# Value products with the values as stationary operand, two heads side by side, in three attention mixers

## The chip, the cores and the metric

The kernel runs on one core of a Trainium2 chip. The metric is the device time of one execution in microseconds. The core has TensorE (PE, matmuls; its weight loads are listed apart as PEld), VectorE (DVE), ScalarE (ACT), GpSimd (POOL) and SyncE (SP, which issues most DMAs). Matmul results land in PSUM banks, from which the other engines read.

## The reference

Two different transformer blocks of two layers each work on 512 tokens with 1024 features, in fp32. The first block has three mixers (sliding-window attention with sinks, HGRN2, mLSTM), the second has three attention mixers: a forgetting attention ("C", 6 heads of 64, a decay per head added to the scores), a differential one ("A", 4 heads of 64 from pairs of scores) and a dilated one ("B", 6 heads of 64). MLPs follow the mixers. The part that the change touches is, in the sliding-window mixer:

```python
    o = jnp.einsum('bnhgqk,bnkhd->bnqhgd', probs.astype(v.dtype), vv)
    return o.reshape(B, S, HQ * d)
```

and the like product of probabilities and values in mixers C and B. Each output is then multiplied by an output projection and added to the residual.

## The kernel before, in words

The residual x lies with features on the partitions, as 8 tiles of 128x512. A projection with weights is taken in three passes of split operands (`mm3`, L176 to L178): every operand is split into a high part and a rest by a ScalarE copy (L136) and a VectorE subtraction (L137). `feat_group` gives results with features on the partitions, `tok_group` with tokens on the partitions. The weights come by DMA from SP's queue.

The attention mixers go by token tiles t of 128 query rows. In mixers C and B a head's scores are one matmul of 64 rows (`softmax_block`, L1089: queries of the tile as stationary operand, keys moving); VectorE adds mask and maximum (L1093), ScalarE takes the exponential (L1094). `pv` (L1095 to L1107) transposes the probabilities in chunks of 128 keys (L1103, bank ps_T), copies them to at_pT (L1105), and then takes, for each chunk, the transposed probabilities (128x128) as stationary operand and 64 value columns as the moving one; the result goes to 64 columns of the bank ps_o, tokens on the partitions:

```python
        for c in range(t + 1):
            nc.tensor.matmul(po, pT[:, c * P:c * P + P], v(c), start=c == 0, stop=c == t)
```

After the last head of a tile one VectorE instruction multiplies ps_o by the reciprocal sums, broadcast over a head's 64 columns (L1164 in C into yc, L1231 in B into yo, L603 in `swa` into ysw). Before an output projection the results are brought to features on the partitions: by `to_feat` (L510 to L520, PE transposes L517, then a split) for ysw, yc and the differential mixer's ya, and by transposes at L1253 for yo. In `swa` two heads share a bank ps_T and one copy (L590 to L593) ahead of their value matmuls (L597). In mixer C, GpSimd loads the decay rows (fg_b, L1153) and adds the causal mask (L1154); the scores wait for that add.

Tile's scheduler sets the order of the instructions on each engine (`schedule_with_timeline_sim=True`, L1518) from the program order, the buffers and its own costs. The bank ps_o has one buffer, ps_T and ps_S two each, ps_mm three. The norms ahead of the next stage are generators whose pieces are woven in: `start` hands one over and `tick` advances it by the work done since (L216 to L236); `attend` in mixer B calls `tick(3000)` for each head.

Of the kernel before, what the change touches and what calls it, by code (L numbers as in the profile page):

```python
# [9 lines left out]
F32 = mybir.dt.float32  # L10
F32R = mybir.dt.float32r
BF16 = mybir.dt.bfloat16
I32 = mybir.dt.int32
# [48 lines left out]
class Builder:  # L62
# [328 lines left out]
    def mixers1(self, l, mp, act, nxt):  # L391
# [105 lines left out]
        sink = lambda m, pt, sl: nc.vector.tensor_tensor(self.x[m][:, sl], self.x[m][:, sl], pt, ALU.add)  # L497
        act = [self.to_feat(X, sub(ysw, i), "mm") for i in range(4)]
        for g in range(2):
# [23 lines left out]
    def swa(self, l, mp, sp, ysw, row):  # L523
# [44 lines left out]
        for t in range(NT):  # L568
# [9 lines left out]
            for j in range(8):  # L578
# [12 lines left out]
                if j % 2 == 1:  # L591
                    pT = sp.tile([P, S], F32, name="sw_pT", tag="sw_pT", bufs=2)
                    nc.scalar.copy(pT[:, :2 * w], tp[:, :2 * w])  # L593
                    for jj in (j - 1, j):
                        for c in range(w // P):
                            o, v = (jj % 2) * w + c * P, 640 + (jj % 2) * 64
                            nc.tensor.matmul(po[:, jj * 64:jj * 64 + 64], pT[:, o:o + P], ysw[k0 // P + c][:, v:v + 64],  # L597
                                             start=c == 0, stop=c == w // P - 1)
            nc.vector.tensor_tensor(es, sinks, mx, ALU.add)
            nc.scalar.activation(es, es, AF.Exp)  # L600
            nc.vector.tensor_tensor(den, den, es, ALU.add)
            nc.vector.reciprocal(den, den)
            nc.vector.tensor_tensor(ysw[t][:, 0:512].rearrange("p (h e) -> p h e", e=64),  # L603
                                    po.rearrange("p (h e) -> p h e", e=64),
                                    den.unsqueeze(2).broadcast_to([P, 8, 64]), ALU.mult)

# [490 lines left out]
    def pv(self, mp, s, t, po, v):  # L1097
# [8 lines left out]
        for c in range(t + 1):  # L1106
            nc.tensor.matmul(po, pT[:, c * P:c * P + P], v(c), start=c == 0, stop=c == t)  # L1107

    def mixers2(self, l, mp, act, nxt):
        nc = self.nc  # L1110
# [34 lines left out]
        for t in reversed(range(NT)):  # L1145
            po = self.ps("o")
            den = mp.tile([P, 6], F32, name="at_den", tag="at_den", bufs=2)
            for i in range(3):
                pair = []
                for h in (2 * i, 2 * i + 1):  # L1150
                    fbt = mp.tile([P, S], F32, name="fg_b", tag="fg_b", bufs=3)
                    w = (t + 1) * P
                    nc.gpsimd.dma_start(fbt[:, :w], fd[0, h * S:h * S + w].partition_broadcast(P))  # L1153
                    nc.gpsimd.tensor_tensor(fbt[:, t * P:w], fbt[:, t * P:w], self.c_caus[:, 3 * P:], ALU.add)  # L1154
                    pair.append(fbt[:, :w])
                ss = []
                for h in (2 * i, 2 * i + 1):
                    b = (h % 2) * 64
                    s, dn = self.softmax_block(mp, qk[i][b:b + 64], qk[3 + i][b:b + 64], t, pair[h % 2], 0.125)
                    nc.vector.reciprocal(den[:, h:h + 1], dn)  # L1160
                    ss.append(s)
                for h in (2 * i, 2 * i + 1):
                    self.pv(mp, ss[h % 2], t, po[:, h * 64:h * 64 + 64], lambda c: yc[c][:, h * 64:h * 64 + 64])
            nc.vector.tensor_tensor(yc[t][:, 0:384].rearrange("p (h e) -> p h e", e=64),  # L1164
                                    po[:, 0:384].rearrange("p (h e) -> p h e", e=64),
                                    den.unsqueeze(2).broadcast_to([P, 6, 64]), ALU.mult)

# [50 lines left out]
        sub = lambda y, i: [y[t][:, i * P:i * P + P] for t in range(NT)]  # L1218
        act = [self.to_feat(X, sub(yc, i)) for i in range(3)] + [self.to_feat(X, sub(ya, i)) for i in range(2)]

        def attend(t):
            po = self.ps("o")
            den = mp.tile([P, 6], F32, name="at_den", tag="at_den", bufs=2)
            for h in range(6):
                b = (h % 2) * 64
                s, dn = self.softmax_block(mp, qkb[h // 2][b:b + 64], qkb[3 + h // 2][b:b + 64], t,
                                           self.c_dil[:, (3 - t) * P:], 0.125)
                nc.vector.reciprocal(den[:, h:h + 1], dn)
                self.pv(mp, s, t, po[:, h * 64:h * 64 + 64], lambda c: yb[c][:, h * 64:h * 64 + 64])
                self.tick(3000)  # L1230
            nc.vector.tensor_tensor(yo[t].rearrange("p (h e) -> p h e", e=64),  # L1231
                                    po[:, 0:384].rearrange("p (h e) -> p h e", e=64),
                                    den.unsqueeze(2).broadcast_to([P, 6, 64]), ALU.mult)

# [6 lines left out]
        for sl in HALVES:  # L1241
# [3 lines left out]
            if wo is None:  # L1245
# [3 lines left out]
                aa = [(self.slot(Y, F32R), self.slot(Y, F32R)) for _ in range(3)]  # L1249
            for i in range(3):  # L1250
                pt = self.ps("T")[:, 0:S // 2]
                for u, t in enumerate(ts):
                    nc.tensor.transpose(pt[:, u * P:u * P + P], yo[t][:, i * P:i * P + P], self.ident)  # L1253
                self.split(aa[i][0][:, sl], aa[i][1][:, sl], pt)
            self.feat_group(wo, 3, 8, aa, sink, 0, (sl,))
# [267 lines left out]
```

## Time and profile before

| | |
|---|---|
| runs | median 2810.25 us of 3 (2807.56 to 2813.39) |
| profiled execution | 2809.55 us, its span 2807.8 us |
| PE busy | 2737.6 us (98%) |
| VectorE, ScalarE, GpSimd busy | 63%, 42%, 8% |
| DMA | 285.59 MB, mean 102 GB/s |

The span is the time from the first to the last instruction of the profiled execution. Busy shares are averages over the span. Matmuls are pipelined: the mean duration of one (some 270 ns for a small one) is longer than the time it takes from the engine, which is read from where the next one starts. A row of a timeline joins matmuls of one kind; its start is that of the first. A matmul with fp32 operands appears as two recorded passes. A shape such as 64*128 behind an operation is the part of the array it takes, rows by columns; 64x512 behind it is the moving operand. In rows of the order, the last shape is partitions by elements of the result's operand.

### The profile page before, as it was taken

How to read it: one execution, taken by the hardware profiler on the slowest of the kernel's cores; microseconds unless marked ns; L12 is line 12 of the kernel's file. 1: busy time of each engine (PE TensorE's matmuls, PEld its weight loads, DVE VectorE, ACT ScalarE, POOL GpSimd, SP SyncE). 2: the span in 40 equal slices, each digit the busy share in tenths (PEclk: the TensorE clock that was granted, in tenths of full speed). 3: DMA queues.
4: the chain of work that ended last, by engine and by line, in shares of the span. 5: the costliest groups of instructions: out<-in, count | busy, mean ns of one | idle time of the engine just before them, and what ended most of it. 6: DMA issues, size and time to landing. Idle time of an engine off the chain costs nothing.

```text
span 2807.8 us, 42599 instructions
## 1 busy us (share of the span) xinstructions
PE 2737.6 (98%) x16360; PEld 2343.3 (83%) x16360; DVE 1777.0 (63%) x3842; ACT 1174.7 (42%) x2294; POOL 235.8 (8%) x606
## 2 busy tenths in 40 slices
PE   8999999999999999999999999999999999999998
PEld 7887887889978788788988788888889777988887
DVE  7677777468667757766754656655554475665555
ACT  4644532226374543232634445433234544532332
POOL 2000100002200010000213100000000410000000
PEclk9998999999999999999999999999999999999999
DMA  4211486332221127733223121223332302133222
GB/s 153 76 48 52 136 263 226 103 104 92 90 72 46 54 98 254 256 130 102 91 83 112 30 72 57 89 86 98 99 105 81 100 23 86 39 105 98 90 89 77
DMA packets 87644, 285.59 MB, mean 102 GB/s; under 512 B 10972, under 2 KB 15132, under 8 KB 87440
## 3 DMA queue, kind: packets, MB, share of 16 engines
q1 hardware_dynamic: 81280, 266.49, 29.3%
q0 software_dynamic: 5872, 16.35, 2.2%
q8 instruction: 128, 2.10, 0.3%
q14 instruction: 76, 0.62, 0.1%
q10 hardware_dynamic: 288, 0.03, 0.0%
HBM read 280.69 MB, written 2.14 MB: 101 GB/s over the span
## 4 chain that ended last, share of the span: by engine, by line
PE 77%; DVE 9%; DMA 7%; issue 2%; ACT 2%; POOL 2%; SPq 0%; DVEq 0%; POOLq 0%; ACTq 0%
PE ps_mm L176 12%; PE ps_mm L177 12%; PE ps_mm L178 12%; DMA wm<-w_mod 5%; PE ps_T L176 5%; PE ps_T L177 5%; PE ps_T L178 5%; PE ps_S L176 5%; PE ps_S L177 5%; PE ps_S L178 5%; PE ps_S L1089 3%; PE ps_o L1107 2%; DVE wm L1032 2%; PE ps_T L1103 1%; DVE wl L137 1%
## 5 line engine op out<-in xcount | busy, mean ns | idle before, releaser
L136 ACT CAST wh<-wr 128x1024 fp32r<-128x1024 f32 (+4 forms) x414 | 407.2, 987 | 661.2 <-PE ps_mm L177 212.3
L137 DVE TENSOR_TENSOR wl<-wr,wh 128x1024 fp32r<-128x1024 f32 (+4 forms) x414 | 472.9, 1143 | 304.0 <-ACT wh L136 296.3
L177 PE MATMUL ps_mm<-slotA,wh 128*128 128x512 f32 (+1 forms) x632 | 229.3, 364 | 3.4 <-DVE slotA L317 2.0
L176 PE MATMUL ps_mm<-slotA,wh 128*128 128x512 f32 (+1 forms) x632 | 226.8, 366 | 1.5 <-ACT slotA L316 0.7
L178 PE MATMUL ps_mm<-slotA,wl 128*128 128x512 f32 (+1 forms) x632 | 226.7, 360 | 0.0
L176 PE MATMUL ps_mm<-wh,slotA 128*128 128x256 f32 (+3 forms) x688 | 207.6, 303 | 0.0
L177 PE MATMUL ps_mm<-wl,slotA 128*128 128x256 f32 (+3 forms) x688 | 206.2, 300 | 0.0
L178 PE MATMUL ps_mm<-wh,slotA 128*128 128x256 f32 (+3 forms) x688 | 205.6, 299 | 0.0
L1032 DVE CUSTOM_DVE_ANT_0 wm<-wm,sc 128x1024 f32<-128x1024 f32 x96 | 117.5, 1224 | 67.9 <-DMA wm<-w_mod 67.4
L136 ACT CAST m_h<-tmp 128x512 fp32r<-128x512 f32 (+1 forms) x122 | 71.4, 587 | 210.3 <-DVE tmp L911 173.9
L176 PE MATMUL ps_mm<-slotB,wh 128*128 128x512 f32 (+1 forms) x408 | 142.5, 359 | 2.6 <-ACT slotB L136 1.6
L177 PE MATMUL ps_mm<-slotB,wh 128*128 128x512 f32 (+1 forms) x408 | 143.6, 353 | 1.4 <-DVE slotB L137 1.4
L176 PEld LDWEIGHTS ps_mm<-wh,slotA 128*128 128x128 f32 x688 | 131.8, 192 | 12.1 <-issue 9.5
L178 PE MATMUL ps_mm<-slotB,wl 128*128 128x512 f32 (+1 forms) x408 | 141.7, 349 | 0.0
L177 PEld LDWEIGHTS ps_mm<-slotA,wh 128*128 128x128 f32 x632 | 122.4, 194 | 22.6 <-issue 3.1
L178 PEld LDWEIGHTS ps_mm<-wh,slotA 128*128 128x128 f32 x688 | 131.3, 191 | 12.0 <-issue 11.4
L176 PEld LDWEIGHTS ps_mm<-slotA,wh 128*128 128x128 f32 x632 | 121.6, 194 | 22.6 <-issue 3.6
L177 PEld LDWEIGHTS ps_mm<-wl,slotA 128*128 128x128 f32 x688 | 131.6, 191 | 10.2 <-issue 8.9
L178 PEld LDWEIGHTS ps_mm<-slotA,wl 128*128 128x128 f32 x632 | 122.5, 194 | 17.5 <-issue 2.6
L176 PE MATMUL ps_S<-m_h,wh 128*128 128x512 f32 (+1 forms) x355 | 129.8, 366 | 3.6 <-DVE yacc L945 3.3
L1094 ACT ACTIVATE at_s<-at_s,at_st 128x512 f32<-128x512 f32 (+3 forms) x160 | 89.5, 560 | 100.0 <-DVE at_st L1093 89.1
L178 PE MATMUL ps_S<-m_h,wl 128*128 128x512 f32 (+1 forms) x355 | 129.4, 365 | 0.0
(628 smaller groups left out, 7291.3 us busy)
## 6 DMA issues: line engine op xcount, KB each, us to landing
wr<-w_up SPq DMA_DIRECT2D x152, 512.0 KB, 3.8
wm<-w_mod SPq DMA_DIRECT2D x96, 512.0 KB, 4.6
wr<-w_dn SPq DMA_DIRECT2D x64, 512.0 KB, 4.0
wr<-w_dn SPq DMA_DIRECT2D x32, 384.0 KB, 3.1
wr<-w_dn SPq DMA_DIRECT2D x32, 320.0 KB, 2.9
wr<-w_f SPq DMA_DIRECT2D x16, 512.0 KB, 3.8
wr<-w_pg SPq DMA_DIRECT2D x16, 512.0 KB, 3.7
wr<-w_t SPq DMA_DIRECT2D x12, 512.0 KB, 4.9
```

The costliest lines, as they stand in the source:

```text
L136: nc.scalar.copy(hi, src)
L137: nc.vector.tensor_tensor(lo, src, hi.bitcast(F32), ALU.subtract)
L176: nc.tensor.matmul(out, ah, bh, start=i == 0, stop=False)
L177: nc.tensor.matmul(out, ah, bl, start=False, stop=False)
L178: nc.tensor.matmul(out, al, bh, start=False, stop=i == n - 1)
L1032: nc.vector.tensor_tensor_reduce(w, w, self.sc, 1.0, 0.0, ALU.mult, ALU.add, accum_out=self.mod[l][:, j:j + 1])
L1089: nc.tensor.matmul(pt, q[:, t * P:w], k[:, 0:w], start=True, stop=True, tile_position=None if row is None else (row, 0))
L1094: nc.scalar.activation(s, s, AF.Exp, bias=st[:, 0:1], scale=-1.0, accum_out=st[:, 1:2])
L1103: nc.tensor.transpose(tp[:, c * P:c * P + P], s[:, c * P:c * P + P], self.ident)
L1107: nc.tensor.matmul(po, pT[:, c * P:c * P + P], v(c), start=c == 0, stop=c == t)
```

## The change

`pv2` takes a pair of heads. It transposes both heads' probabilities and copies them, then takes for each chunk the values (128 keys x 64) as stationary operand and the transposed probabilities (128 keys x 128 tokens) as the moving one. The first head's result goes to partitions 0 to 63 of ps_o, the second's to 64 to 127 (`tile_position=(0, u * 64)`), so that the results have features on the partitions. `out_scaled` spreads the reciprocal sums over 64 columns a head (GpSimd, into tmp), transposes them into a bank ps_T, copies them back (ScalarE) and multiplies ps_o by them (VectorE). `parts_of` splits the results in pieces of 128x128 without transposes. Mixers C and B and `swa` use these; the differential mixer keeps `pv`. In B the transposes of the tail (L1253) go, the heads are taken in pairs, and `tick` is called once for each pair. Line numbers in the rows of the changed order are those of the changed file: L175 to L177 there are L176 to L178 before, L1086 is L1089, L580 is L581, L589 is L590, L1064 is L1067, L1186 and L1187 are L1153 and L1154.

```diff
@@ -495,7 +494,7 @@
 
         sub = lambda y, i: [y[t][:, i * P:i * P + P] for t in range(NT)]
         sink = lambda m, pt, sl: nc.vector.tensor_tensor(self.x[m][:, sl], self.x[m][:, sl], pt, ALU.add)
-        act = [self.to_feat(X, sub(ysw, i), "mm") for i in range(4)]
+        act = [self.parts_of(X, ysw, i) for i in range(4)]
         for g in range(2):
             self.feat_group(self.wload("w_oa1", l * 2 + g, 4 * 512), 4, 4, act, sink, 4 * g)
         self.hgrn_out(gg)
@@ -591,18 +590,16 @@
                 if j % 2 == 1:
                     pT = sp.tile([P, S], F32, name="sw_pT", tag="sw_pT", bufs=2)
                     nc.scalar.copy(pT[:, :2 * w], tp[:, :2 * w])
-                    for jj in (j - 1, j):
-                        for c in range(w // P):
-                            o, v = (jj % 2) * w + c * P, 640 + (jj % 2) * 64
-                            nc.tensor.matmul(po[:, jj * 64:jj * 64 + 64], pT[:, o:o + P], ysw[k0 // P + c][:, v:v + 64],
-                                             start=c == 0, stop=c == w // P - 1)
+                    for c in range(w // P):
+                        for u in range(2):
+                            o, v = u * w + c * P, 640 + u * 64
+                            nc.tensor.matmul(po[u * 64:u * 64 + 64, f * P:f * P + P], ysw[k0 // P + c][:, v:v + 64],
+                                             pT[:, o:o + P], start=c == 0, stop=c == w // P - 1, tile_position=(0, u * 64))
             nc.vector.tensor_tensor(es, sinks, mx, ALU.add)
             nc.scalar.activation(es, es, AF.Exp)
             nc.vector.tensor_tensor(den, den, es, ALU.add)
             nc.vector.reciprocal(den, den)
-            nc.vector.tensor_tensor(ysw[t][:, 0:512].rearrange("p (h e) -> p h e", e=64),
-                                    po.rearrange("p (h e) -> p h e", e=64),
-                                    den.unsqueeze(2).broadcast_to([P, 8, 64]), ALU.mult)
+            self.out_scaled(ysw[t][:, 0:512], po, den, 4)
 
 
     def hgrn(self, l, mp, yf, yhi):
@@ -1106,6 +1103,42 @@
         for c in range(t + 1):
             nc.tensor.matmul(po, pT[:, c * P:c * P + P], v(c), start=c == 0, stop=c == t)
 
+    def pv2(self, mp, ss, t, po, v):
+
+        nc = self.nc
+        w = (t + 1) * P
+        pTs = []
+        for s in ss:
+            tp = self.ps("T")
+            for c in range(t + 1):
+                nc.tensor.transpose(tp[:, c * P:c * P + P], s[:, c * P:c * P + P], self.ident)
+            pT = mp.tile([P, S], F32, name="at_pT", tag="at_pT", bufs=3)[:, :w]
+            nc.scalar.copy(pT, tp[:, :w])
+            pTs.append(pT)
+        for c in range(t + 1):
+            for u, pT in enumerate(pTs):
+                nc.tensor.matmul(po[u * 64:u * 64 + 64], v(c, u), pT[:, c * P:c * P + P], start=c == 0, stop=c == t,
+                                 tile_position=(0, u * 64))
+
+    def out_scaled(self, dst, po, rden, n):
+
+        nc = self.nc
+        pr = self.ps("T")
+        rb = self.tmp()[:, 0:n * P]
+        nc.gpsimd.tensor_copy(rb.rearrange("p (h e) -> p h e", e=64), rden.unsqueeze(2).broadcast_to([P, 2 * n, 64]))
+        for i in range(n):
+            nc.tensor.transpose(pr[:, i * P:i * P + P], rb[:, i * P:i * P + P], self.ident)
+        nc.scalar.copy(rb, pr[:, 0:n * P])
+        nc.vector.tensor_tensor(dst, po[:, 0:n * P], rb, ALU.mult)
+
+    def parts_of(self, which, ys, i):
+
+        h, lo = self.slot(which, F32R), self.slot(which, F32R)
+        for t in range(NT):
+            tt = slice(t * P, t * P + P)
+            self.split(h[:, tt], lo[:, tt], ys[t][:, i * P:i * P + P])
+        return h, lo
+
     def mixers2(self, l, mp, act, nxt):
         nc = self.nc
         X, Y = "A", "B"
@@ -1146,24 +1179,20 @@
             po = self.ps("o")
             den = mp.tile([P, 6], F32, name="at_den", tag="at_den", bufs=2)
             for i in range(3):
-                pair = []
+                pair, ss = [], []
                 for h in (2 * i, 2 * i + 1):
                     fbt = mp.tile([P, S], F32, name="fg_b", tag="fg_b", bufs=3)
                     w = (t + 1) * P
                     nc.gpsimd.dma_start(fbt[:, :w], fd[0, h * S:h * S + w].partition_broadcast(P))
                     nc.gpsimd.tensor_tensor(fbt[:, t * P:w], fbt[:, t * P:w], self.c_caus[:, 3 * P:], ALU.add)
                     pair.append(fbt[:, :w])
-                ss = []
                 for h in (2 * i, 2 * i + 1):
                     b = (h % 2) * 64
                     s, dn = self.softmax_block(mp, qk[i][b:b + 64], qk[3 + i][b:b + 64], t, pair[h % 2], 0.125)
                     nc.vector.reciprocal(den[:, h:h + 1], dn)
                     ss.append(s)
-                for h in (2 * i, 2 * i + 1):
-                    self.pv(mp, ss[h % 2], t, po[:, h * 64:h * 64 + 64], lambda c: yc[c][:, h * 64:h * 64 + 64])
-            nc.vector.tensor_tensor(yc[t][:, 0:384].rearrange("p (h e) -> p h e", e=64),
-                                    po[:, 0:384].rearrange("p (h e) -> p h e", e=64),
-                                    den.unsqueeze(2).broadcast_to([P, 6, 64]), ALU.mult)
+                self.pv2(mp, ss, t, po[:, i * P:i * P + P], lambda c, u: yc[c][:, (2 * i + u) * 64:(2 * i + u) * 64 + 64])
+            self.out_scaled(yc[t][:, 0:384], po, den, 3)
 
         qka = [self.slot(Y) for m in range(4)]
         for g in range(2):
@@ -1216,21 +1245,22 @@
         w = self.wload("w_bv2", l, 8 * 384, parts=4)
         self.tok_group(w, 8, 384, act, lambda t, pt: nc.scalar.copy(yb[t], pt))
         sub = lambda y, i: [y[t][:, i * P:i * P + P] for t in range(NT)]
-        act = [self.to_feat(X, sub(yc, i)) for i in range(3)] + [self.to_feat(X, sub(ya, i)) for i in range(2)]
+        act = [self.parts_of(X, yc, i) for i in range(3)] + [self.to_feat(X, sub(ya, i)) for i in range(2)]
 
         def attend(t):
             po = self.ps("o")
             den = mp.tile([P, 6], F32, name="at_den", tag="at_den", bufs=2)
-            for h in range(6):
-                b = (h % 2) * 64
-                s, dn = self.softmax_block(mp, qkb[h // 2][b:b + 64], qkb[3 + h // 2][b:b + 64], t,
-                                           self.c_dil[:, (3 - t) * P:], 0.125)
-                nc.vector.reciprocal(den[:, h:h + 1], dn)
-                self.pv(mp, s, t, po[:, h * 64:h * 64 + 64], lambda c: yb[c][:, h * 64:h * 64 + 64])
-                self.tick(3000)
-            nc.vector.tensor_tensor(yo[t].rearrange("p (h e) -> p h e", e=64),
-                                    po[:, 0:384].rearrange("p (h e) -> p h e", e=64),
-                                    den.unsqueeze(2).broadcast_to([P, 6, 64]), ALU.mult)
+            for i in range(3):
+                ss = []
+                for h in (2 * i, 2 * i + 1):
+                    b = (h % 2) * 64
+                    s, dn = self.softmax_block(mp, qkb[i][b:b + 64], qkb[3 + i][b:b + 64], t,
+                                               self.c_dil[:, (3 - t) * P:], 0.125)
+                    nc.vector.reciprocal(den[:, h:h + 1], dn)
+                    ss.append(s)
+                self.pv2(mp, ss, t, po[:, i * P:i * P + P], lambda c, u: yb[c][:, (2 * i + u) * 64:(2 * i + u) * 64 + 64])
+                self.tick(6000)
+            self.out_scaled(yo[t], po, den, 3)
 
         yo = [self.slot(X)[:, 0:384] for t in range(NT)]
         wo = None
@@ -1247,11 +1277,10 @@
                     self.feat_group(self.wload("w_oa2", l * 4 + g, 5 * 256), 5, 2, act, sink, 2 * g)
                 wo = self.wload("w_ob2", l, 3 * 1024, parts=3)
                 aa = [(self.slot(Y, F32R), self.slot(Y, F32R)) for _ in range(3)]
-            for i in range(3):
-                pt = self.ps("T")[:, 0:S // 2]
-                for u, t in enumerate(ts):
-                    nc.tensor.transpose(pt[:, u * P:u * P + P], yo[t][:, i * P:i * P + P], self.ident)
-                self.split(aa[i][0][:, sl], aa[i][1][:, sl], pt)
+            for t in ts:
+                tt = slice(t * P, t * P + P)
+                for i in range(3):
+                    self.split(aa[i][0][:, tt], aa[i][1][:, tt], yo[t][:, i * P:i * P + P])
             self.feat_group(wo, 3, 8, aa, sink, 0, (sl,))
             self.start(nxt(sl))
```

**First place:** PE in mixer C of the first layer of the second block, at the last token tile, where ps_o takes value products, ps_T transposes, ps_S scores, and ps_mm is a projection woven in. Before:

```order
L176 MATMUL ps_mm<-wh,slotA 128x256
L1107 MATMUL ps_o<-yc_14478,at_pT 128x64
L1107 MATMUL ps_o<-yc_14479,at_pT 128x64
L1107 MATMUL ps_o<-yc_14480,at_pT 128x64
L1107 MATMUL ps_o<-yc_14481,at_pT 128x64
L1103 MATMUL ps_T<-ident,at_s 128x128 x4
L1089 MATMUL ps_S<-slotB 128x512 x2
L177 MATMUL ps_mm<-wl,slotA 128x256
```

The same place in the changed program:

```order
L177 MATMUL ps_mm<-wh,slotA 128x256
L1120 MATMUL ps_o<-at_pT,yc_14550 64x128
L1120 MATMUL ps_o<-at_pT,yc_14551 64x128 x2
L1120 MATMUL ps_o<-at_pT,yc_14552 64x128 x2
L1120 MATMUL ps_o<-at_pT,yc_14553 64x128 x2
L1114 MATMUL ps_T<-ident,at_s 128x128 x4
L1120 MATMUL ps_o<-at_pT,yc_14550 64x128
L1114 MATMUL ps_T<-ident,at_s 128x128 x4
L1086 MATMUL ps_S<-slotB 128x384 x2
```

The two heads' matmuls of a chunk now follow each other, in a run of seven; the eighth, the first head's first, had gone ahead, as it does for the next pair: alone, between the transposes of that pair's two heads.

**Second place:** PE in `swa` of the first layer of the first block, at a token tile with two chunks of keys. Before:

```order
L177 MATMUL ps_mm<-wl,slotA 128x264
L597 MATMUL ps_o<-ysw_205,sw_pT 128x64 x2
L581 MATMUL ps_S<-sw_q_765,slotB 128x256
L178 MATMUL ps_mm<-wh,slotA 128x264
L590 MATMUL ps_T<-ident,sw_s 128x128 x2
```

The same place in the changed program:

```order
L176 MATMUL ps_mm<-wl,slotA 128x264
L580 MATMUL ps_S<-sw_q_765,slotB 128x256
L596 MATMUL ps_o<-sw_pT,ysw_205 64x128 x2
L596 MATMUL ps_o<-sw_pT,ysw_206 64x128 x2
L177 MATMUL ps_mm<-wh,slotA 128x264
L175 MATMUL ps_mm<-wh,slotA 128x264
L589 MATMUL ps_T<-ident,sw_s 128x128 x2
```

Here the four value matmuls of a pair of heads stand together, chunk by chunk.

**Third place:** POOL in mixer C, where fg_b is the decay row of a head and rp_a belongs to the differential mixer's rotary embedding. Before:

```order
L1153 DMA fg_b<-fg_d_14626 128x384
L1154 TENSOR_TENSOR fg_b<-fg_b,c_caus 128x128 x2
L1153 DMA fg_b<-fg_d_14626 128x384 x2
L1067 TENSOR_TENSOR rp_a<-rp_a,rp_b 128x256
L1154 TENSOR_TENSOR fg_b<-fg_b,c_caus 128x128 x2
```

The same place in the changed program:

```order
L1186 DMA fg_b<-fg_d_14698 128x384
L1187 TENSOR_TENSOR fg_b<-fg_b,c_caus 128x128
L1128 COPY tmp<-at_den 128x384
L1187 TENSOR_TENSOR fg_b<-fg_b,c_caus 128x128
L1186 DMA fg_b<-fg_d_14698 128x384 x2
L1064 TENSOR_TENSOR rp_a<-rp_a,rp_b 128x256
```

The copy that spreads the reciprocals of one token tile stands between the mask adds for the next.

## Rows read from the trace of the kernel before

**Rows 1.** The page: busy time by engine, and the last chain by engine.

```profile
PE 2737.6 (98%) x16360; PEld 2343.3 (83%) x16360; DVE 1777.0 (63%) x3842; ACT 1174.7 (42%) x2294; POOL 235.8 (8%) x606
...
PE 77%; DVE 9%; DMA 7%; issue 2%; ACT 2%; POOL 2%; SPq 0%; DVEq 0%; POOLq 0%; ACTq 0%
```

**Rows 2.** Waits of PE: what, on whom: us in total, times, longest.

```profile
PE ps_S L176 <- ACT wh L136: 9.8, 3, 7.6
...
PE ps_o L1107 <- ACT at_pT L1105: 0.7, 2, 0.3
```

**Rows 3.** Groups of instructions on PE: xcount, busy us, mean ns, idle before.

```profile
L1107 PE MATMUL ps_o<-yb,at_pT 128*128 128x64 f32 x240 | 32.5, 271 | 1.0 <-ACT at_pT L1105 0.7 <-DVE slotA L1231 0.3
L1107 PE MATMUL ps_o<-yc,at_pT 128*128 128x64 f32 x240 | 29.8, 269 | 0.0
L597 PE MATMUL ps_o<-ysw,sw_pT 128*128 128x64 f32 x224 | 29.0, 270 | 0.0
```

**Rows 4.** Chain that ended last, mixer B: start us, us, what.

```profile
1686.78 1.29 PE ps_o L1107 x12
```

**Rows 5.** Timeline of PE in hgrn: start us, us, instruction, xcount.

```profile
172.53 0.39 PE L679 MATMUL ps_o<-yhi,hg_kt 128*128 128x128 f32 x2
172.75 0.49 PE L789 MATMUL ps_T<-ident,yg 128*4 128x128 f32 x3
```

**Rows 6.** Timeline of PE, 64x64 tiles in a long run and alone.

```profile
198.26 1.30 PE L733 MATMUL ps_S<-tmp 64*64 64x64 f32 x34
...
201.59 0.33 PE L733 MATMUL ps_S<-tmp 64*64 64x64 f32 x2
```

**Rows 7.** Timeline of PE around one transpose of four rows.

```profile
190.25 0.28 PE L176 MATMUL ps_mm<-wh,slotA 128*128 128x256 f32 x1
190.46 0.22 PE L811 MATMUL ps_T<-ident,ml_P 4*128 4x4 f32 x1
...
190.84 0.28 PE L178 MATMUL ps_mm<-wh,slotA 128*128 128x256 f32 x1
```

**Rows 8.** Timeline of PE around one transpose onto six columns.

```profile
1486.12 0.28 PE L176 MATMUL ps_mm<-wh,slotA 128*128 128x256 f32 x1
1486.24 0.28 PE L177 MATMUL ps_mm<-wl,slotA 128*128 128x256 f32 x1
1486.36 0.27 PE L1130 MATMUL ps_o<-ident,yc 128*6 128x128 f32 x1
1486.39 0.37 PE L177 MATMUL ps_mm<-wl,slotA 128*128 128x256 f32 x1
1486.59 0.28 PE L178 MATMUL ps_mm<-wh,slotA 128*128 128x256 f32 x1
```

**Rows 9.** Timelines of PE around score products L1089 in mixer B.

```profile
1671.71 0.39 PE L176 MATMUL ps_mm<-slotA,wh 128*128 128x512 f32 x1
1671.94 0.39 PE L177 MATMUL ps_mm<-slotA,wh 128*128 128x512 f32 x1
1672.26 0.70 PE L1089 MATMUL ps_S<-slotB 64*128 64x256 f32 x2
...
1673.22 0.39 PE L176 MATMUL ps_mm<-slotA,wh 128*128 128x512 f32 x1
...
1710.21 1.12 PE L1089 MATMUL ps_S<-slotB 64*128 64x512 f32 x2
...
1722.51 1.13 PE L1089 MATMUL ps_S<-slotB 64*128 64x512 f32 x4
```

**Rows 10.** Groups on GpSimd and ScalarE: xcount, busy us, mean ns, idle before.

```profile
L1067 POOL TENSOR_TENSOR rp_a<-rp_a,rp_b 128x256 f32<-128x256 f32 x40 | 32.8, 822 | 241.0 <-DVE rp_b L1066 153.7 <-DVE df_c L1194 41.0 <-PE ps_S L1089 18.6
L1154 POOL TENSOR_TENSOR fg_b<-fg_b,c_caus 128x128 f32<-128x128 f32 x48 | 22.1, 463 | 52.3 <-DMA fg_b<-fg_d 51.6
L1105 ACT COPY at_pT<-ps_T 128x384 f32<-128x384 f32 x32 | 14.6, 475 | 19.5 <-PE ps_T L1103 19.5
```

**Rows 11.** Busy time in a window: us, PE, PEld, DVE, ACT, POOL, PEclk, DMA, GB/s.

```profile
1698.20:1708.40 10.20, 10.20 (x35) 7.40 (x36) 2.79 (x12) 3.27 (x11) 0.00 (x0) 0.50 0.08 28
```

More of the change, by code (lines that the diff above doesn't have):

```diff
@@ L11 @@
 F32R = mybir.dt.float32r
-BF16 = mybir.dt.bfloat16
 I32 = mybir.dt.int32
```

## Prediction

> **What bounds the kernel now.** I read the page first [rows 1]: PE is busy 2737.6 of the span's 2807.8 us, VectorE 63%, ScalarE 42%, GpSimd 8%, and 77% of the chain that ended last lies on PE. Then PE's waits [rows 2]: the longest group is 9.8 us in the whole run, and the value matmuls waited for their transposed probabilities for 0.7 us in all. So the kernel issues on PE nearly all the time, and an edit is worth what it saves or adds in PE's own stream, unless it makes a new wait. The value matmuls of the three mixers are 240, 240 and 224 recorded passes [rows 3], 704 in all (two passes to one fp32 matmul). Their mean of 270 ns is the latency of one; they overlap. The price of a pass is its share of a stretch: twelve took 1.29 us on the chain [rows 4], 0.1075 each.
>
> **Removed: the old value passes.** 704 x 0.1075 = **-75.7 us**. A pass streams only 64 columns but holds a full 128x128 stationary operand.
>
> **Added: the new value passes.** The orders hold the same 352 matmuls, so 704 passes, now with a 128x64 stationary and 128 moving columns. A pass of 128 moving columns alone costs 0.11: two L679 passes lead to the next row 0.22 us later [rows 5] (172.53 to 172.75). Two heads stand side by side in the array. No row shows that shape, the nearest is the hgrn product L733, 64x64 tiles: two lone passes take 0.33 us, 34 passes take 1.30 [rows 6], so the other 32 add 0.97, 0.030 each, against 0.1075 for a full-array pass of 64 columns. Passes on different tiles therefore run beside one another. With two column tiles I take half, 0.056 a pass: 704 x 0.056 = **+39.4**. Bounds: 0.053 (half of 0.1075) and 0.11 (no overlap, a rival below).
>
> **Passes without a partner.** The changed order on PE hoists the first matmul of head 0 to where its probabilities are copied, before head 1 is there (first order place of the change). I count 119 runs of 128x64 tiles: 32 in the sliding-window mixer, 24 of four and 8 of two, all paired (second place), and 87 in the second block: 47 of one matmul and 31 others of odd length (12 of three, 10 of five, 9 of seven). 78 matmuls thus have no partner; each costs a half more on its two passes, 2 x 0.055 = 0.11: **+8.6**.
>
> **Lost pairs of score products.** L1089 takes 64 rows; two neighbours on different row halves run together: at 512 columns four passes take 1.13 us and two take 1.12 [rows 9]. By the order the pairs go from 50 to 40 (64 rows) and from 8 to 6 (32 rows), 12 pairs less, so 12 excursions more. One at 256 columns: from 1671.94 to 1673.22 are 1.28 us over two steps that take 0.23 each (1671.71 to 1671.94) [rows 9], 0.82. 12 x 0.8 = **+9.6**; between 0.4 (at 128 columns, the product itself being a third) and 1.1 (512 columns) 5 to 13.
>
> **Fewer excursions in hgrn.** The scheduler groups the 64x64 products better: 33 entries from the full array become 18. What one costs is seen at L811, a transpose of 4 rows among 128-row matmuls: from L176 at 190.25 to L178 at 190.84 are 0.59 us [rows 7], for two steps of 0.12 (1486.12 to 1486.24, [rows 8]); 0.35, of which I leave 0.02 to its own four columns. 15 x 0.33 = **-5.0** (-5 to 0, as the order on the chip may wait elsewhere).
>
> **Transposes.** 80 go (24 and 32 of L517, 24 of L1253), 80 come (spread reciprocals), all 128x128: **0** on PE.
>
> **The new chain behind each token tile.** Before, one VectorE multiply emptied the bank ps_o. Now, 24 times, a GpSimd copy spreads the reciprocals, PE transposes them, ScalarE copies them back, then VectorE multiplies. GpSimd took 463 ns for an add at 128x128 and 822 at 128x256 [rows 10], 0.36 per further 128 columns, so about 1.2 us at 128x384 (an estimate; a copy has one input less); the ScalarE copy took 0.475 [rows 10]. The bank and its result come 1.65 us later. In the forgetting mixer the copies also stand in GpSimd's queue between the loads of fg_b and the mask adds (third place), where the next tile's scores wait for those adds. If all 24 stood on the path, 24 x 1.65 = 40; if PE has other work, 0. PE's queue puts weight matmuls between, and the like hand-over today costs 0.7 [rows 2]; the places with least cover are the ends of the two dilated halves in each of two layers. I take **+4**, two to three of the 24.
>
> **At nothing.** ScalarE gets 24 copies (24 x 0.475 = 11 us [rows 10]), and it and VectorE the splits as 80 pieces of 128x128 in place of 26 larger ones: the same elements in more instructions. ScalarE is at 42%, VectorE at 63%, and PE's stream covers both; without that cover the dilated ends would show it, within the term above. No DMA is added or removed; SP issues the same transfers with a few neighbours swapped, so the weights come as before. The tick per pair moves the pre-norm pieces by half a pair, no work.
>
> **Sum.** -75.7 + 39.4 + 8.6 + 9.6 - 5.0 + 4 = -19.1. The profiled execution took 2809.55 (0.7 below the median of 2810.25), so 2790.4; I forecast **2790 us**. This case's own range is 2780 (no new wait, cheap lost pairs) to 2802 (nine tiles' chains exposed).
>
> **Does a change of columns drain the array?** The order counts 661 changes of the array's shape between matmuls, 465 before. In this trace the drain shows where the number of rows changes [rows 7, 9]. Where only columns change it does not: the transpose onto 6 columns at 1486.36 between two weight matmuls [rows 8] makes 1486.24 to 1486.59 last 0.35 instead of 0.24, and 0.11 is the price of its own 128 moving columns; L789 onto 4 columns stands beside L679 at 0.11 a pass [rows 5]. I take no drain for 128x64. But those rows ask for 6 and 4 columns at column 0 of the array; nothing shows a tile that begins at column 64.
>
> **Rival 1, slower: the column tiles drain like the row tiles.** Of the 119 runs' ends, 95 entries come from the full array and 113 exits go to it (the rest border on row tiles, which drain anyway): 208 switches, 104 trips x 0.33 = +34.3, so -19.1 + 34.3 = +15: **2825** (2815 to 2832, at 0.24 to 0.40 a trip). The gain is gone from 0.18 a trip. For it: a tile that begins at column 64 is as much a tile of its own as one that begins at row 64. Against it: [rows 5, 8]. Chance 0.28.
> The Trainium skill, page "TensorEngine Tiling (Array Packing)", section Tiling Modes, lists 128x64 as a mode of its own and says that "changing tiling mode (not just tile) drains the TensorE"; by that rule this rival's sum holds, and the trace agrees for rows and does not for fewer columns at column 0.
>
> **Rival 2, the change does not do what it says:** the column tiles don't run side by side. Then 704 x 0.11 = 77.4 stands in place of 39.4 + 8.6, 29.4 more: +10, about **2820**, without drains. For it: only tiles that differ in rows also take different partitions of the moving operand; here both take all 128. Against it: 0.030 in [rows 6] is nearer a quarter of 0.1075 than a half, so columns too run beside each other there. Chance 0.05.
>
> **Rival 3: the new chain decides.** Half of the 24 tiles expose their 1.65 us, 20 in place of 4, and the stretch at half clock in the dilated second half (10.2 us at 0.50 [rows 11]) grows by the pauses: about **2808**. For it: one ps_o bank, GpSimd in a row with DMA issues. Against it: the scheduler placed other PE work between. Chance 0.07.
>
> **How the numbers follow.** Main case 0.60. A measurement here tells about 0.2% from no change, 5.6 us: 2804 to 2816. Faster: nearly all of the main case and a bit of rival 3, 0.59. Same: rival 3, the main case's upper end and rival 1's lower, 0.10. Slower: rivals 1 and 2, 0.31. The range 2778 to 2826 holds the main case, rivals 2 and 3 and over half of rival 1.
>
> **What would show it.** Right: value rows 64x128 in runs of four passes lasting about 0.22 us beyond one pass; weight matmuls around them at their usual step plus the passes' share; waits of PE on ps_T behind GpSimd or on ps_o of a few us in all. Rival 1: 0.3 us more around each run. Rival 2: passes 0.11 apart in both halves. Rival 3: "POOL tmp" or "DVE yc" high among PE's waits. The forecast is wrong if the weight matmuls around a run are late by more than the passes explain.

## The result and the profile after

The changed kernel took 2878.93 us (median of 4 runs, 2875.6 to 2879.35) where the kernel before took 2809.65: 1.0242 times, 95% interval 1.0225 to 1.026. It is 69 us slower. The forecast was 2790, its range ended at 2826, and the dearest rival stood at 2825.

The page of the changed kernel, busy time by engine, against [rows 1]:

```profile
PE 2780.4 (97%) x16360; PEld 2345.0 (82%) x16360; DVE 1781.7 (62%) x3896; ACT 1194.1 (42%) x2372; POOL 247.8 (9%) x630
...
PE 78%; DVE 9%; DMA 6%; ACT 3%; POOL 2%; issue 2%; SPq 0%; DVEq 0%; ACTq 0%; POOLq 0%
```

Nothing here names a cause: PE is busy 43 us more with as many passes. The span and the mean granted clock of TensorE do, before and then after:

```profile
core 0: 2807.8 us, clock 0.984
```

```profile
core 0: 2877.1 us, clock 0.965
```

Span times (1 - clock) is 44.9 us before and 100.7 after. Up to 56 of the 69 us are therefore PE at its lower level of 1.2 GHz. Where it was is shown by the page's line of 40 slices of 72 us: two dips to 5, where the line of the kernel before has one slice at 8 and none lower:

```profile
PEclk9995999999999589999999999999999999999999
```

The first is the hgrn and mLSTM part of the first layer. Windows there, after (us, busy PE, PEld, DVE, ACT, POOL, PEclk, DMA share, GB/s):

```profile
210.00:230.00 20.00, 13.62 (x220) 11.78 (x221) 19.84 (x44) 6.87 (x11) 2.56 (x4) 0.80 0.25 81
230.00:250.00 20.00, 15.77 (x159) 11.74 (x156) 15.22 (x24) 10.06 (x22) 0.00 (x0) 0.50 0.00 1
250.00:270.00 20.00, 20.00 (x74) 15.57 (x73) 3.96 (x8) 6.92 (x18) 2.42 (x4) 0.50 0.09 26
270.00:290.00 20.00, 17.24 (x66) 14.31 (x65) 12.29 (x47) 7.57 (x22) 0.69 (x1) 0.50 0.00 1
```

The same stretch before, from 20 us earlier on:

```profile
190.00:210.00 20.00, 17.07 (x276) 15.45 (x274) 19.84 (x44) 7.61 (x12) 2.85 (x4) 1.00 0.26 83
210.00:230.00 20.00, 20.00 (x131) 15.60 (x130) 14.61 (x22) 8.85 (x16) 0.00 (x0) 0.83 0.16 53
230.00:250.00 20.00, 20.00 (x110) 15.46 (x110) 11.70 (x21) 12.29 (x29) 2.44 (x4) 1.00 0.24 79
```

VectorE is busy 19.84 of 20 us in hgrn, before and after. What PE did ahead of the fall of the clock, in the first layer (L177 is a weight pass, L676 and L730 are hgrn's):

```profile
217.66 0.39 PE L177 MATMUL ps_mm<-slotA,wl 128*128 128x512 f32 x1
217.89 0.38 PE L676 MATMUL ps_o<-yhi,hg_kt 128*128 128x128 f32 x2
218.64 0.76 PE L730 MATMUL ps_S<-tmp 64*64 64x64 f32 x18 [0.37 <-DVE slotB L737]
```

The weight pass at 217.66 us is followed by none until 292.8. The clock fell to 0.5 at 222.1 us, after 1.0 us of idle time from 218 on, and stayed there for 72 us; most of the 6.4 us that PE idled in the first window came after the fall. In the second layer the weight passes pause from 945.4 to 1026.1 us, and the clock is at 0.5 for 78 us from 949.1 on. Whether the want of work took the clock down is tested below. PE's waits (us in all, times, longest) show hgrn's products L730 and the mLSTM's L865 and L853, where the kernel before waited 0.5 us at the first of these lines (L733 there), 0.5 at the second (L868) and not at the third:

```profile
PE ps_S L730 <- DVE slotB L737: 8.2, 4, 5.9
...
PE ps_S L730 <- DVE slotA L737: 7.7, 4, 6.0
...
PE ps_T L865 <- DVE ml_P L860: 5.5, 2, 2.8
PE ps_S L853 <- DVE ml_P L860: 4.3, 2, 2.2
PE ps_T L1130 <- POOL tmp L1128: 4.2, 1, 4.2
```

The last line is the new spread chain: one wait of 4.2 us. Why hgrn came late is seen on VectorE. Its preparation begins with an operation into a tmp buffer (L635 before, L632 after). Before, then after:

```profile
70.36 0.69 DVE L635 SCALAR_TENSOR_TENSOR tmp<-slotB 128x512 f32<-128x512 f32 x1
```

```profile
160.11 0.20 DVE L601 RECIPROCAL sw_den<-sw_den 128x8 f32<-128x8 f32 x1
160.23 0.64 DVE L632 SCALAR_TENSOR_TENSOR tmp<-slotB 128x512 f32<-128x512 f32 x1
```

It moved by 90 us, to right behind the reciprocals of the last token tile of `swa`. The order says what follows: with 123 of hgrn's 274 matmuls issued, 163 weight passes were still to come before the mLSTM's last product in the kernel before; after, 14 were left, and none from hgrn's 133rd matmul on. PE had spent its filling work while hgrn waited.

The new value passes themselves, in mixer C (start us, us, xcount), against a 0.12 step of the weight passes [rows 8]:

```profile
1577.31 0.28 PE L176 MATMUL ps_mm<-wl,slotA 128*128 128x256 f32 x1
1577.43 0.28 PE L177 MATMUL ps_mm<-wh,slotA 128*128 128x256 f32 x1
1577.64 1.09 PE L1120 MATMUL ps_o<-at_pT,yc 128*64 128x128 f32 x14
1578.66 0.44 PE L1114 MATMUL ps_T<-ident,at_s 128*128 128x128 f32 x2
```

Entry takes 0.21 instead of 0.12. In the trace partners start 0.007 us apart and pairs 0.109 apart. The 14 passes are six pairs and one matmul without a partner, whose two passes take a step each: eight steps, 0.87. From 1577.43 to 1578.66 are 1.23, so 0.24 is left behind the weight pass's 0.12; and the second transpose starts 0.164 behind the first instead of 0.109. The trip to the column tiles and back thus costs 0.29, the drain that [rows 7] show for rows at about the same price. The 59 runs of the trace that stand at full clock between full-array passes, with a pass of 128 columns behind, have a median of 0.29. A run of four among weight passes of 256 columns in `swa`:

```profile
90.71 0.28 PE L175 MATMUL ps_mm<-wh,slotA 128*128 128x256 f32 x1
90.92 0.44 PE L596 MATMUL ps_o<-sw_pT,ysw 128*64 128x128 f32 x4
91.29 0.39 PE L176 MATMUL ps_mm<-wl,slotA 128*128 128x256 f32 x1
91.51 0.28 PE L177 MATMUL ps_mm<-wh,slotA 128*128 128x256 f32 x1
```

0.80 from 90.71 to 91.51, less 0.24 for the two weight passes and 4 x 0.0545 for two pairs, leaves 0.34.

### The profile page after: what moved, and what is told of

It is laid out like the page before. It is cut to its first block, busy times and chain, and to the rows that moved or that the text cites. A ratio compares the mean times of both kernels' runs of the same rounds, so it can differ in the third digit from the quotient of the medians.

```text
span 2877.1 us, 42842 instructions
## 1 busy us (share of the span) xinstructions
PE 2780.4 (97%) x16360; PEld 2345.0 (82%) x16360; DVE 1781.7 (62%) x3896; ACT 1194.1 (42%) x2372; POOL 247.8 (9%) x630
## 4 chain that ended last, share of the span: by engine, by line
PE 78%; DVE 9%; DMA 6%; ACT 3%; POOL 2%; issue 2%; SPq 0%; DVEq 0%; ACTq 0%; POOLq 0%
PE ps_mm L175 12%; PE ps_mm L177 12%; PE ps_mm L176 12%; DMA wm<-w_mod 5%; PE ps_T L175 5%; PE ps_T L176 5%; PE ps_T L177 5%; PE ps_S L175 5%; PE ps_S L177 5%; PE ps_S L176 5%; PE ps_S L1086 3%; DVE wm L1029 2%; PE ps_o L1120 2%; PE ps_T L1114 1%; PE ps_S L580 1%
## 5 line engine op out<-in xcount | busy, mean ns | idle before, releaser
L176 PE MATMUL ps_mm<-slotA,wh 128*128 128x512 f32 (+1 forms) x632 | 225.2, 358 | 2.0 <-DVE slotA L316 2.0
L175 PE MATMUL ps_mm<-slotA,wh 128*128 128x512 f32 (+1 forms) x632 | 224.1, 360 | 1.7 <-ACT slotA L315 0.7
L177 PE MATMUL ps_mm<-slotA,wl 128*128 128x512 f32 (+1 forms) x632 | 224.1, 356 | 0.0
L175 PE MATMUL ps_mm<-wh,slotA 128*128 128x256 f32 (+3 forms) x688 | 209.0, 304 | 0.0
L177 PE MATMUL ps_mm<-wh,slotA 128*128 128x256 f32 (+3 forms) x688 | 208.2, 303 | 0.0
L176 PE MATMUL ps_mm<-wl,slotA 128*128 128x256 f32 (+3 forms) x688 | 206.5, 301 | 0.0
L177 PEld LDWEIGHTS ps_mm<-wh,slotA 128*128 128x128 f32 x688 | 132.1, 192 | 17.2 <-issue 16.1
L175 PE MATMUL ps_mm<-slotB,wh 128*128 128x512 f32 (+1 forms) x408 | 141.8, 353 | 4.1 <-ACT slotB L135 3.3
L175 PEld LDWEIGHTS ps_mm<-wh,slotA 128*128 128x128 f32 x688 | 132.2, 192 | 15.7 <-issue 11.9
L176 PE MATMUL ps_mm<-slotB,wh 128*128 128x512 f32 (+1 forms) x408 | 141.1, 347 | 2.0 <-DVE slotB L136 2.0
L177 PE MATMUL ps_mm<-slotB,wl 128*128 128x512 f32 (+1 forms) x408 | 140.1, 344 | 0.0
L176 PEld LDWEIGHTS ps_mm<-wl,slotA 128*128 128x128 f32 x688 | 132.3, 192 | 9.3 <-issue 8.0
L176 PEld LDWEIGHTS ps_mm<-slotA,wh 128*128 128x128 f32 x632 | 120.6, 191 | 20.7 <-DVE slotA L316 2.9
L175 PEld LDWEIGHTS ps_mm<-slotA,wh 128*128 128x128 f32 x632 | 119.9, 192 | 19.5 <-DVE x L496 1.5
L177 PEld LDWEIGHTS ps_mm<-slotA,wl 128*128 128x128 f32 x632 | 120.4, 190 | 16.3 <-issue 1.0
L175 PE MATMUL ps_S<-m_h,wh 128*128 128x512 f32 (+1 forms) x355 | 129.5, 365 | 3.5 <-DVE yacc L942 3.2
L177 PE MATMUL ps_S<-m_h,wl 128*128 128x512 f32 (+1 forms) x355 | 129.2, 364 | 0.0
```

What stands on the lines that cost most here:

```text
L175: nc.tensor.matmul(out, ah, bh, start=i == 0, stop=False)
L176: nc.tensor.matmul(out, ah, bl, start=False, stop=False)
L177: nc.tensor.matmul(out, al, bh, start=False, stop=i == n - 1)
```

## The experiments

Every ratio is to the kernel before, run beside it on the same chip. The median of the kernel before lay between 2803.61 and 2809.65 us in the five groups of runs, so times of runs from different groups differ by up to 6 us for that alone, and their ratios are the better comparison.

**Is the shared tmp buffer what moved hgrn?** Two runs from opposite sides. One (inplace1) writes the spread reciprocals of `swa` into the output tile, whose query columns are no longer needed:

```diff
-            self.out_scaled(ysw[t][:, 0:512], po, den, 4)
+            self.out_scaled(ysw[t][:, 0:512], po, den, 4, ysw[t][:, 0:512])
...
-        rb = self.tmp()[:, 0:n * P]
+        rb = self.tmp()[:, 0:n * P] if rb is None else rb
```

> The changed kernel, but in the sliding-window mixer the spread reciprocals are written into the output tile itself instead of a tmp buffer. Theory A (the four shared tmp buffers are handed out in program order, so hgrn's first tmp had to wait for the last tile's spread copy; hgrn's preparation came 90 us later, the projections that fill PE beside hgrn were used up before, and PE fell to half clock): preparation back near 70 us, half clock back to a few short stretches, 2879 less about 56, 2815 to 2828. Theory B (the half clock comes from the new value products and the earlier end of the mixer themselves): stays at 2865 to 2880.

Measured: 1.0084 (1.0051 to 1.0118), 2826.98 us. Theory B falls. The time is at the upper end of theory A's range; against the kernel before it is 23 us more, where theory A left 5 to 18. Two stretches at half clock, of 30.7 us each, are left (see below). hgrn's preparation is back:

```profile
71.84 0.68 DVE L632 SCALAR_TENSOR_TENSOR tmp<-slotB 128x512 f32<-128x512 f32 x1
```

The other (dummy_tmp) adds a write to a tmp buffer to the kernel before and nothing else:

```diff
             nc.vector.reciprocal(den, den)
+            nc.gpsimd.tensor_copy(self.tmp()[:, 0:8], den)
```

> The kernel before, with one addition: at the end of each token tile of the sliding-window mixer GpSimd writes the reciprocals (128x8) into a tmp buffer that nobody reads. Theory A: hgrn's preparation goes behind the last tile, long half clock stretches near 230 and 960 us, 2860 to 2885 with the old value products throughout. Theory B: four small GpSimd instructions a layer, 2808 to 2813.

Measured: 1.0069 (1.0046 to 1.0092), 2824.64 us; the preparation went to 151.24 us, again right behind the last reciprocals:

```profile
151.12 0.20 DVE L602 RECIPROCAL sw_den<-sw_den 128x8 f32<-128x8 f32 x1
151.24 0.64 DVE L636 SCALAR_TENSOR_TENSOR tmp<-slotB 128x512 f32<-128x512 f32 x1
151.45 0.48 POOL L603 COPY tmp<-sw_den 128x8 f32<-128x8 f32 x1 [20.88 <-ACT tmp L654]
```

Theory A holds in kind: four tiny writes a layer cost 20 us. Note that L636 starts before the copy: it did not wait for the data on the chip; the scheduler had put it there on VectorE's queue. That it hands out the buffers of a pool in program order fits both runs; the rule itself was not looked at. In size theory A came out 30 us or more too high (the longest half clock stretch is 51 us, in the second layer): here 96 weight passes were left in the first layer when hgrn had 156 of its matmuls, so less of the end was bare.

**Does PE's clock fall because it has too little to do there?** The changed kernel gets work that nobody needs (after_warm):

```diff
                 pt = self.ps("S")
+                for _ in range(4):
+                    nc.tensor.matmul(pt[:, 0:P], self.ident, self.ones, start=True, stop=True)
...
                 pt = self.ps("ST"[j % 2])[:, :w]
+                for _ in range(4):
+                    nc.tensor.matmul(pt[:, 0:P], self.ident, self.ones, start=True, stop=True)
```

> The changed kernel with 128 idle fp32 matmuls a layer of the first block (four of 128x128 into each bank ps_S or ps_T ahead of the hgrn and mLSTM score products, which overwrite them): 28 us of PE work a layer at full clock. Theory G (PE falls to half clock because it has too little to do beside hgrn and the mLSTM): the half clock stretches of 71.7 and 78.5 us shrink to under 20 each and give back 25 to 35 a layer, part of the added work lies in PE's idle time: between 25 less and 10 more than the changed kernel. Theory H (the clock falls for another reason): the stretches stay, and the added work costs 40 to 100 more in all.

> The changed kernel once more, beside after_warm on the same chip: 1.024 times the kernel before.

Measured: 2864.88 us against 2876.13 for the changed kernel on the same chip (1.0222, 1.0205 to 1.0239, against 1.0268, 1.0252 to 1.0283). With 256 matmuls more the kernel is 11 us faster, and the stretches are gone. The changed kernel beside it, then this run:

```profile
core 0: 2874.2 us, clock 0.964
```

```profile
core 0: 2863.9 us, clock 0.991
```

512 passes at 0.11 are 56 us; by span times (1 - clock) the clock gave back the difference of 103.5 and 25.8, 78. That leaves 22; 11 to 13 came. Theory G, within its bounds. The added work also changed the order: with half of hgrn's own matmuls issued, 39 weight passes were still to come in the first layer and 14 in the second, where the changed kernel had none. So the run shows that PE with more to do beside hgrn keeps its clock; it does not tell the idle matmuls from the weight passes that stayed with them.

**What does the second block cost by itself?** In block2_only, `swa` as before, `pv2`, `out_scaled` and `parts_of` in mixers C and B alone.

> The changed second block with the first block as before. Theory C (the column tiles drain PE, about 0.25 to 0.33 us a trip, 87 runs in the second block): 240+240 passes save 24.7, lone passes and lost score pairs cost 18, drains 22 to 29, some waits: 2822 to 2835, hgrn at full clock. Theory D (no drain): 2803 to 2809.

Measured: 1.0054 (1.0032 to 1.0076), 2816.88 us: 0.5% slower, where the forecast's sum without drains gives a gain. The time is a little below theory C's range, but the kernel before ran 6 us faster here than where the forecast started, and the 13 to 15 us above it are what theory C has (12 to 25). From the first VectorE instruction of `mixers2` (the memset of fg_one) to that of `mlp2`, both layers, the traces give 641.2 us before and 654.1 here.

**Are drains and lone passes the price?** In rev_u the second head of a chunk comes first, so nothing can go ahead of its copy:

```diff
-            for u, pT in enumerate(pTs):
+            for u, pT in reversed(list(enumerate(pTs))):
```

> As inplace1, and in pv2 the second head of a chunk comes first, so that no matmul can go ahead of the other head's copy: 82 runs of column tiles in place of 119, and 4 matmuls without a partner in place of 78. Theory C (drain): against inplace1 37 trips x 0.3 = 11 less and 74 x 0.11 = 8 less, so about 19 less, near 2800. Theory D (no drain): 8 less only.

Measured: 1.0002 (0.9986 to 1.0019), 2803.64 us, 23 less than inplace1. A pair of heads with four chunks is now one run of 16 passes, and takes what 14 took:

```profile
1521.04 0.28 PE L176 MATMUL ps_mm<-wl,slotA 128*128 128x256 f32 x1
1521.25 1.09 PE L1120 MATMUL ps_o<-at_pT,yc 128*64 128x128 f32 x16
1522.27 0.66 PE L1114 MATMUL ps_T<-ident,at_s 128*128 128x128 f32 x4
```

Again 1.23 from the weight pass to the transpose: eight pairs take the eight steps that six pairs and a lone matmul took, and the trip of the matmul that had gone ahead is saved.

The 23 us can't be put down to drains and lone passes alone, because the edit also brought score products back side by side. Counted in the traces, the scores of the second block stand in 118 runs before, in 128 in inplace1 and in 116 here. At the prediction's 0.8 us each, the 12 runs less are worth 10 us. With the 8 of the lone passes, 18 would come without any drain, and 29 with 37 trips at 0.29. The measured 23 lies between, so this run does not decide about the drain; the rows above and the run with the full array do.

The same edit without the new `swa` (block2_rev):

> First block as before, second block changed with the second head of a chunk first. 37 runs of column tiles less and 74 lone matmuls less than block2_only. If drains and lone passes cost what rev_u showed against inplace1 (23 less), 2794, 10 less than before; if that gain came from elsewhere in rev_u, 2817.

Measured: 0.9971 (0.9958 to 0.9983), 2798.63 us: **0.3% faster than the kernel before**, the only run that is. The stage measured above takes 632.2 us in both layers, 9.0 less than before and 21.9 less than block2_only. Its ends in the first layer, before, then here:

```profile
1431.82 0.06 DVE L1134 MEMSET fg_one<- 6x1 f32 x1
1751.18 0.41 DVE L1280 TENSOR_SCALAR tmp<-c_g,conv 128x256 f32<-128x256 f32 x1
```

```profile
1428.47 0.06 DVE L1169 MEMSET fg_one<- 6x1 f32 x1
1741.82 0.41 DVE L1311 TENSOR_SCALAR tmp<-c_g,conv 128x256 f32<-128x256 f32 x1
```

The other traces agree: the stage takes 641 to 646 us with the old second block (three traces), 654 to 660 with the changed one (six), and 632 to 635 with the second head first (three). The gain on the kernel before, 5 us by the medians and 8 by the ratio, is less than the 10 expected.

**The drain by taking the column tiles away.** The same matmuls on the full array, with the 128 value columns of both heads as stationary operand (`v` now gives these); each output also holds the other head's product:

```diff
-                nc.tensor.matmul(po[u * 64:u * 64 + 64], v(c, u), pT[:, c * P:c * P + P], start=c == 0, stop=c == t,
-                                 tile_position=(0, u * 64))
+                nc.tensor.matmul(po, v(c, 0), pT[:, c * P:c * P + P], start=c == 0 and u == 0, stop=c == t and u == 1)
```

> block2_only, but the stationary operand of each value matmul is the 128 value columns of both heads, and both heads add up in the same 128 partitions: the same 240 matmuls in the same loops, all on the full array, with no change of columns (each output also holds the other head's product, so the output isn't the reference's). No pass runs beside another: 480 x 0.1075 = 52 in place of 480 x 0.056 + 87/119 of the drain. Theory C (drain about 0.33 a trip, some 72 trips of the second block not beside a row tile): the 17 to 25 that pairing saved are lost and 24 of drains are gone: 0.999 to 1.006 times before, where block2_only is 1.0054. Theory D (no drain): 1.011 to 1.014.

Measured: 1.0009 (0.9995 to 1.0022), 2809.88 us, inside theory C's range and clear of theory D's. Fourteen passes take 14 steps instead of eight, entry and exit cost nothing:

```profile
1513.28 0.28 PE L177 MATMUL ps_mm<-wh,slotA 128*128 128x256 f32 x1
1513.40 1.73 PE L1122 MATMUL ps_o<-at_pT,yc 128*128 128x128 f32 x14
1514.96 0.49 PE L1116 MATMUL ps_T<-ident,at_s 128*128 128x128 f32 x3
```

1.68 from the weight pass to the transpose, 0.12 + 14 x 0.11. The scores stand in 128 runs, as in block2_only. Some 17 us of side by side running were given up and the kernel got no slower: 5 us less in the stage (649.4), 13 by the ratios. So the drains of the second block are worth 22 to 30 us, 0.25 to 0.34 for each of 87 runs, which holds the 0.29 and 0.34 read from the rows.

**What remains in the first block?** The new `swa` of inplace1 with the second block as before (swa_only):

> The first block of inplace1, the second as before. Theory E: the half clock stretches near 254 and 961 us stay, the value products save, net about +10 on the kernel before (the difference of inplace1 and block2_only). If the effects of the two blocks don't add: anything else; the forecast without clock and drain would be 10 less than before.

Measured: 1.0034 (1.0021 to 1.0047), 2813.05 us, the 10 of theory E, and two stretches at half clock of 30.7 us, in the mLSTM's end, as in inplace1. Twenty passes L865 in inplace1 take 4.53 us there; before, 18 of the same took 2.22 (L868):

```profile
251.09 4.53 PE L865 MATMUL ps_T<-yv,ml_P 128*128 128x66 f32 x20
```

```profile
256.40 2.22 PE L868 MATMUL ps_T<-yv,ml_P 128*128 128x66 f32 x18
```

By the order 11 weight passes were left in inplace1 with 20 of the mLSTM's 72 products done, 59 before. Putting the removed transposes back (redo_transp; the attention output is then in the wrong layout) brings them back, 68 by the order:

```diff
-        act = [self.parts_of(X, ysw, i) for i in range(4)]
+        act = [self.to_feat(X, sub(ysw, i), "mm") for i in range(4)]
```

> inplace1, with the 32 transposes ahead of the first block's attention output projection put back (they now transpose what is already transposed, so the attention output is wrong in its layout; the work is that of inplace1 plus 32 transposes). Theory E (without those transposes the projection w_oa1 runs earlier, nothing is left for PE beside the end of the mLSTM, and PE falls to half clock there, 30.7 us in each layer): by the order 68 weight passes instead of 11 are left when a quarter of the mLSTM's products is done; the half clock stretches near 254 and 961 us go, 19 less than inplace1 less 3.5 for the transposes, 2806 to 2817 where inplace1 is 2827. Theory F (the stretch belongs to the new value products): 2827 to 2833.

Measured: 1.0061 (1.0041 to 1.0081), 2822.43 us. In place of the stretches of 30.7 us, 6.8 us near 265 and 10.2 near 965 us are left (with 13.7 near 204, new here), and the mean clock rose from 0.979, so theory F falls:

```profile
core 0: 2818.6 us, clock 0.985
```

But only 5 us came (6 by the ratios), where 15 were expected: span times (1 - clock) fell from 59.3 to 42.3, the transposes took 3.5, and some 8 us are not accounted for. The difference of the two ratios is uncertain by 0.4%, 11 us, so these 8 us are not clear of the noise; part of that stretch may also have waited anyway. This stays open.

An attempt to keep the filling work by other buffers missed:

```diff
-        act = [self.parts_of(X, ysw, i) for i in range(4)]
+        act = [self.parts_of(dict(X=X, Y=Y)["XXYY"[i]], ysw, i) for i in range(4)]
```

> rev_u, with two of the four split pieces of the first block's attention output taken from the buffers that the mLSTM uses, so that their projection comes later: by the order 48 weight passes are left for the last 52 of the mLSTM's 72 product groups, none beside hgrn's last third. Theory E: the stretch in the mLSTM's end shortens, 2804 less about 10; if the bare hgrn part falls to half clock instead, 2800 to 2820.

Measured: 1.0067 (1.0043 to 1.0092), 2825.86 us, worse than rev_u and above both forecasts. The work was saved for the mLSTM's end and taken from hgrn's: in the first layer the clock is at half for 47.8 us from 215 us on.

## Why the prediction was wrong

**Right.** The bound outside hgrn: PE's stream. The old passes, 0.1075 each, and the new ones: pairs run side by side at 0.0545 a pass, so rival 2 falls. The 78 matmuls without a partner and the lone runs, from the order. The lost pairs of score products in kind; the traces have 10 excursions more (118 to 128), not 12. That the new spread chain cost what the sum gave it is luck: the term of 4 meant two or three chains of 1.65, and PE's one wait of 4.2 us is a single chain, whose GpSimd copy took 1.88 us. The copy of 128x384 took 0.51 us in the median, less than half of the 1.2 estimated.

**Wrong: "I take no drain for 128x64".** A trip to the column tiles costs 0.29 to 0.34 us, near the 0.33 of rival 1; its 104 trips are 30 to 35 us, which would have moved the sum from -19 to between +11 and +16. The rows that I set against it [rows 5, 8] have fewer columns that begin at column 0; they did not bear on two tiles that begin at 0 and 64, as the text itself noted before it gave them the greater weight. The Trainium skill's page "TensorEngine Tiling (Array Packing)", section Tiling Modes, has the rule that a change of tiling mode drains the engine. The trace of after agrees, at 0.29 to 0.34 us a trip; [rows 8], a transpose onto six columns at column 0, shows no drain.

**Wrong: "At nothing", and "PE's queue puts weight matmuls between".** Both took the weight passes as cover that is always there, and the shares of the whole span, VectorE at 63%, hid a stage in which VectorE is busy 19.84 of 20 us and PE lives on that cover. The changed order showed otherwise, and I read it as a gain: "33 entries from the full array become 18" in hgrn, -5.0, was the sign that hgrn's products stood bare of weight passes. Nothing in the sum asked what `out_scaled` allocates: its `tmp` is one of four buffers that the next stage also uses, and this alone tied hgrn to the end of `swa`. dummy_tmp shows it without any of the change, at 20 us; inplace1 takes 44 us away by it going by the ratios, 52 by the medians.

**Wrong in kind: rival 3.** It had the clock and the chain, but in the dilated mixer and at 2808. The clock fell in a stage that the change does not compute in: up to 56 us by span times (1 - clock). In both layers it fell right behind the last weight pass, and after_warm shows that it stays up when PE has more to do.

The sum as measured: 69 us by the medians and spans; up to 56 from the clock in hgrn and the mLSTM, 13 for the rest, in which the second block's mixers are 18.4 (641.2 to 659.6) and the sliding-window part a saving. The parts overlap, since PE also idles in the stretches at half clock.

## What to carry to other kernels

A scratch buffer from a shared pool is an edge in the schedule: where buffers are handed out in program order, a late user holds back later allocations, on engines that never touch the data. Before costing work "hidden behind PE", count from the changed order how many filling passes are left at each point of the serial stages that follow. Column tiles paid only in long runs here: a pair of passes saves 0.11 us against the full array and a trip costs 0.29 to 0.34, so a run needs about three pairs to break even, and a matmul that goes ahead alone undoes it.

## What was not expected of the hardware

Added idle matmuls made the kernel faster, 2876.13 to 2864.88 us with 256 of them, as the granted clock rose from 0.964 to 0.991 (with weight passes that moved beside them). And the larger part of a stretch at half clock that was taken away (30.7 us in each layer, redo_transp against inplace1) gave back 5 us net, some 8 without the transposes put back for it, where span times (1 - clock) says 17; the noise does not rule the 17 out.
